# An encoder layer on one core: attention in a written TensorE order by quarters of a head, projections handed out product by product, some normalisations on ScalarE

## The chip, the cores and the metric

The kernel runs on one core of a Trainium2 chip. The time is device microseconds of one execution; the median of three runs of the kernel before is 2068.36 us (2068.29 to 2068.67).

## The reference

Two sequences (`x_prompt`, `x_sample`, here the first and the second stream) of 512 tokens by 1024 channels pass one encoder layer with the same weights: half a SwiGLU feed-forward, a mixing block, another half feed-forward, a last RMSNorm. The mixing block normalises and projects once, runs grouped-query attention and a bidirectional mLSTM side by side, and merges the two by sigmoid gates. What the change touches is the attention and what is computed between its steps:

```python
proj = h @ w_in
aq = apply_rope(rms_norm(aq.reshape(B, S, ATT_HEADS, ATT_HEAD_DIM), q_norm), cos, sin)
ak = apply_rope(rms_norm(ak.reshape(B, S, ATT_KV_HEADS, ATT_HEAD_DIM), k_norm), cos, sin)
...
s = jnp.einsum('bqkgd,bskd->bkgqs', qi, k, preferred_element_type=jnp.float32) * scale
p = jax.nn.softmax(s, axis=-1).astype(v.dtype)
return jnp.einsum('bkgqs,bskd->bqkgd', p, v)
...
merged = jax.nn.sigmoid(g_att) * (att @ w_up_att) + jax.nn.sigmoid(g_mlstm) * (mem @ w_up_mlstm)
```

There are 8 heads of 64 channels, 2 key and value heads, and blocks of 128 queries, so a head has four blocks (0 to 3).

## The kernel before, in words

All of it is float32, made of two float32r halves (a rounded high part and a remainder): a product is three TensorE matmuls (high by high, high by low, low by high) of 128x128 weights by 512 columns. Instructions are recorded in program order; a scheduler then sets the order on each engine from priorities and its own reckoning of when operands are ready, and writes the semaphores. Each engine then runs its list strictly in that order. A few instructions are pinned: they keep the order in which they were recorded (`pin`).

The first feed-forward comes first, then the mixing of both streams (`mix`, a generator that is advanced alternately for the two), then the second feed-forward. In `mix`, `tok_proj` makes keys, values and gates (`kv_done`) and queries (`q_done`), with four PSUM banks at a time: three of the pool MM and the one of PO. `rope_apply` rotates keys and queries on VectorE (DVE); its product with the sine is done in two halves, one for even and one for odd elements (L820). Then follows the attention, head by head:

- `scores(h)`: for each query block, two matmuls into a bank of PS (two banks; L1017), the row maximum on DVE (TENSOR_REDUCE, L1020), the exponential with its row sum on ScalarE (ACT, L1022), a reciprocal and a multiplication of the 128x512 block by it on DVE (L1023, L1024).
- `attend(h)`: for each block of keys, four TensorE transposes into a bank of PT (two banks; L1036), a split into high part (ACT) and remainder (DVE, L671 and L672), and two matmuls with the values into the one bank of PO (L1044); at the end of the head the two halves of PO are added (L1052, L1053).

`scores(h + 1)` is recorded ahead of `attend(h)`. After each head, `fill` hands out one or two units of other work: a projection of 24 matmuls (`proj`, L770), the eight gates of the attention (`att_gate`) and two gates of the mLSTM (`out_gate`), with the load of the next unit's weights ahead of it. In the first stream a weight is split on arrival (L238 on ACT, L239 on DVE) and parked in HBM; in the second stream it comes back split. Each unit ends with a multiplication on DVE and a Tanh on ACT (L1061, L1062). One projection of the mLSTM (`mem_qk(1, 1)`, 24 matmuls) is still held when the attention starts. `extra`, a column sum and a broadcast for the other stream's norm (L202, L212), is recorded once after the third head.

## Time and profile before

| | us |
|---|---|
| median of three runs | 2068.36 |
| the profiled execution, its own time | 2070.33 |
| its span (first to last instruction) | 2068.5 |
| TensorE matmul (PE) busy | 2055.0 |
| TensorE weight load (PEld) busy | 1689.1 |
| VectorE (DVE) busy | 1544.2 |
| ScalarE (ACT) busy | 903.6 |
| GpSimd (POOL) busy | 100.8 |

A record of a matmul lasts from its issue to its modelled end and overlaps the next one, so PE looks busy through short waits. They are found in two other ways: by the number of matmuls in a stretch against the pace of an undisturbed one, and by the idle time of the weight loader, whose records don't overlap. PE is held by a wait at the weight load of the instruction that waits.

### The profile page before, as it was taken

What the parts mean: (1) busy time and instruction counts of PE and PEld (TensorE: products, weight loads), DVE (VectorE), ACT (ScalarE), POOL (GpSimd) and SP (SyncE); (2) the same over time, 40 slices, a digit from 0 to 9 for tenths busy, and PEclk for the clock granted to TensorE, in tenths of its full rate; (3) what the DMA queues carried; (4) which work ended last, traced back from release to release, by engine and by line L of the source; (5) the groups of instructions that cost most, each with busy time, mean ns of one, the idle gap of its engine ahead of it and who ended that gap; (6) DMA issues with size and microseconds to landing.
All of it is one profiled execution on the core that took longest, in us unless ns stands there. A gap on an engine that the chain in (4) does not pass through costs nothing.

```text
span 2068.5 us, 27129 instructions
## 1 busy us (share of the span) xinstructions
PE 2055.0 (99%) x9453; PEld 1689.1 (82%) x9453; DVE 1544.2 (75%) x2784; ACT 903.6 (44%) x1650; POOL 100.8 (5%) x117
## 2 busy tenths in 40 slices
PE   9999999999999999999999999999999999999998
PEld 7888888888888777888877788888888888888887
DVE  7888988786797897575567646545888888795797
ACT  7544444442235566463345443324544444443224
POOL 0000000001003001000120000002000000000001
PEclk9999999999999999999999999999999999999999
DMA  9565655699766645767684345677656555599753
GB/s 323 175 195 172 223 171 185 203 351 347 263 228 248 202 151 186 261 231 271 204 286 162 106 150 190 205 250 249 203 172 215 187 180 183 178 338 355 271 204 120
DMA packets 307240, 454.84 MB, mean 220 GB/s; under 512 B 19976, under 2 KB 179808, under 8 KB 305824
## 3 DMA queue, kind: packets, MB, share of 16 engines
q1 hardware_dynamic: 305104, 447.39, 64.1%
q0 software_dynamic: 1840, 5.46, 0.8%
q8 instruction: 74, 1.21, 0.2%
q14 instruction: 62, 0.51, 0.1%
q10 hardware_dynamic: 160, 0.27, 0.0%
HBM read 286.15 MB, written 166.89 MB: 219 GB/s over the span
## 4 chain that ended last, share of the span: by engine, by line
PE 96%; DVE 1%; DMA 1%; ACT 1%; issue 0%; SPq 0%; ACTq 0%; DVEq 0%
PE mm L770 20%; PE pst L332 12%; PE pso L332 12%; PE mm L332 10%; PE mm L588 8%; PE pss L332 6%; PE pss L588 4%; PE pst L588 4%; PE mm L754 4%; PE pso L588 3%; PE pso L1044 1%; PE pss L1017 1%; PE pso L754 1%; PE pst L1036 1%; PE pso L1180 1%; PE pst L770 1%
## 5 line engine op out<-in xcount | busy, mean ns | idle before, releaser
L770 PE MATMUL mm<-xh,w 128*128 128x512 f32 x896 | 290.4, 394 | 0.0
L332 PE MATMUL pst<-xc,w 128*128 128x512 f32 x1056 | 253.9, 389 | 0.0
L332 PE MATMUL mm<-xc,w 128*128 128x512 f32 x984 | 233.0, 390 | 1.0 <-ACT f L1383 1.0
L332 PEld LDWEIGHTS pst<-xc,w 128*128 128x128 f32 x1056 | 198.0, 188 | 41.7 <-ACT t L367 0.6
L332 PEld LDWEIGHTS mm<-xc,w 128*128 128x128 f32 x984 | 184.2, 188 | 39.4 <-ACT f L1383 1.4
L770 PEld LDWEIGHTS mm<-xh,w 128*128 128x128 f32 x896 | 167.7, 188 | 33.5
L588 PE MATMUL mm<-rt,w 128*128 128x512 f32 x765 | 178.8, 389 | 0.0
L770 PE MATMUL mm<-xl,w 128*128 128x512 f32 x448 | 176.3, 393 | 0.0
L588 PEld LDWEIGHTS mm<-rt,w 128*128 128x128 f32 x765 | 143.6, 188 | 29.8
L290 ACT ACTIVATE w<-t 128x512 fp32r<-128x512 f32 x176 | 107.3, 629 | 135.5 <-issue 55.2
L291 DVE TENSOR_TENSOR w<-t,w 128x512 fp32r<-128x512 f32 x176 | 118.5, 689 | 53.3 <-ACT w L290 51.2
L332 PE MATMUL pso<-xc,f 128*128 128x512 f32 x528 | 126.8, 389 | 0.0
L332 PE MATMUL pss<-xc,w 128*128 128x512 f32 x528 | 126.8, 389 | 0.0
L332 PE MATMUL pso<-xc,w 128*128 128x512 f32 x528 | 126.8, 389 | 0.0
L332 PEld LDWEIGHTS pso<-xc,f 128*128 128x128 f32 x528 | 99.1, 188 | 20.6
L332 PEld LDWEIGHTS pss<-xc,w 128*128 128x128 f32 x528 | 99.1, 188 | 20.6
L332 PEld LDWEIGHTS pso<-xc,w 128*128 128x128 f32 x528 | 99.1, 188 | 20.6
L671 ACT ACTIVATE w<-wr 128x512 fp32r<-128x512 f32 x72 | 45.2, 634 | 138.1 <-PE pso L588 70.2
L671 ACT ACTIVATE w<-t 128x512 fp32r<-128x512 f32 x82 | 51.9, 634 | 107.2 <-PE pst L588 62.4
L770 PEld LDWEIGHTS mm<-xl,w 128*128 128x128 f32 x448 | 84.3, 188 | 16.7
L588 PE MATMUL pss<-rt,w 128*128 128x512 f32 x396 | 93.7, 389 | 0.0
L588 PE MATMUL pst<-rt,w 128*128 128x512 f32 x396 | 93.7, 389 | 0.0
(385 smaller groups left out, 3818.0 us busy)
## 6 DMA issues: line engine op xcount, KB each, us to landing
rt<-rbuf SPq DMA_DIRECT2D x154, 512.0 KB, 5.7
wpark<-w SPq DMA_DIRECT2D x104, 512.0 KB, 3.5
w<-wpark SPq DMA_DIRECT2D x104, 512.0 KB, 4.6
wr<-in_ffn_w_gate_dram SPq DMA_DIRECT2D x62, 512.0 KB, 5.3
rbuf<-tab SPq DMA_DIRECT2D x102, 256.0 KB, 4.0
wr<-in_ffn_w_up_dram SPq DMA_DIRECT2D x44, 512.0 KB, 4.4
rbuf<-f SPq DMA_DIRECT2D x72, 256.0 KB, 4.0
wr<-in_w_in_dram SPq DMA_DIRECT2D x36, 512.0 KB, 5.8
```

Of the source, the lines that this page charges most:

```text
L290: pin(nc.scalar.activation(t[:, 0], src, AF.Copy))
L291: pin(V_.tensor_tensor(t[:, 1], src, f(t[:, 0]), op=ALU.subtract))
L332: nc.tensor.matmul(p, a[:, k, :], xt[:, b, k, :], start=(first and k == 0 and i == 0), stop=(k == HK_ - 1 and i == 2), skip_group_check=True)
L588: nc.tensor.matmul(p, u[:, a, d * P:(d + 1) * P], r[:, b, ts], start=(first and q == 0 and k == 0), stop=(q == len(us) - 1 and k == 2), sk ...
L671: nc.scalar.activation(hi, src, AF.Copy)
L754: nc.tensor.matmul(p[b][:, :N], a[:, k, bs], w_[:, kl, :], start=(k == 0 and i == 0), stop=(k == KD - 1 and i == 2))
L770: nc.tensor.matmul(p, a[:, k, :], b, start=(k == 0 and i == 0), stop=(k == n - 1 and i == 2))
L1017: nc.tensor.matmul(p, qT[:, h, b * P:(b + 1) * P], kv[:, hk * 2 + j, :], start=(j == 0), stop=(j == 1))
L1036: nc.tensor.transpose(p[:, b * P:(b + 1) * P], Ps[b][:, kb * P:(kb + 1) * P], ident)
L1044: nc.tensor.matmul(po, Vst[:, kv_, hk, :], w, start=(kv_ == 0 and i == 0), stop=(kv_ == 3 and i == 1))
L1180: nc.tensor.matmul(po, vm[:, a, t, hs_], b, start=(t == 0 and n == 0), stop=(t == 3 and n == 2))
```

## The change

- The attention is written as quarters of a head. In each quarter TensorE gets: the two score matmuls of one block of the next head, 5 filler matmuls, the four transposes of one key block, 3 filler matmuls, the two value matmuls of the key block before. All are pinned, so TensorE keeps this order; instructions that are not pinned may still stand between them.
- The projections are handed out matmul by matmul (`steps`, `among`) and not in units of 24. The first head's four scores have 9 fillers each. The ten units of the queue hold 240 matmuls; in the first stream the held projection is worked off ahead of the attention (`fill(1)`), in the second it is the first filler, which makes 264. At the end, what is left of the queue is done as before.
- In the first stream, the multiplication by the reciprocal goes to ACT for the odd blocks, 16 in all.
- The sine product of `rope_apply` is one instruction over a reversed pair, no longer two.
- `tok_proj` gets its banks as an argument: PS, PS, MM, MM for keys and values, MM, PO, MM, MM for queries.
- `extra` is split in two: column sums in the third head, broadcast in the fourth.

```diff
     def proj(view, key, src, n, done):
-        return (lambda: load_w(view, key)), (lambda w: done(proj_w(*w, src, n)))
+        def comp(w):
+            done(proj_w(*w, src, n))
+        def steps(w):
...
+                pin(nc.tensor.matmul(p[0], a[:, k, :], b, start=(k == 0 and i == 0), stop=(k == n - 1 and i == 2)))
+                if k == n - 1 and i == 2:
+                    done(p[0])
+            return [lambda k=k, i=i: step(k, i) for k in range(n) for i in range(3)]
...
+    FILLER = 5,3
+    FIRST = 9
...
-                for e in range(2):
-                    V_.tensor_tensor(v5(m)[:, bb, :, :, e], v5(n)[:, bb, :, :, 1 - e],
-                                     s4[:, bb, :, e].unsqueeze(1).to_broadcast([P, hn_, DA // 2]), op=ALU.mult)
+                V_.tensor_tensor(v5(m)[:, bb], v5(n)[:, bb, :, :, ::-1],
+                                 s4[:, bb].unsqueeze(1).to_broadcast([P, hn_, DA // 2, 2]), op=ALU.mult)
...
-        go(*tok_proj(xh, xl, [(512, 256), (2304, 16)], 2, kv_done))
+        go(*tok_proj(xh, xl, [(512, 256), (2304, 16)], 2, kv_done, (PS, PS, MM, MM)))
...
-        go(*tok_proj(xh, xl, [(0, 512)], 2, q_done), mem_qk(0, 0))
+        go(*tok_proj(xh, xl, [(0, 512)], 2, q_done, (MM, PO, MM, MM)), mem_qk(0, 0))
...
+        def score(h, b):
...
+                pin(nc.tensor.matmul(p, qT[:, h, b * P:(b + 1) * P], kv[:, hk * 2 + j, :],
+                                     start=(j == 0), stop=(j == 1)))
...
+            if b % 2 and not s:
+                nc.scalar.activation(e, e, AF.Copy, scale=c[:, 2:3])
+            else:
+                V_.tensor_scalar(e, e, c[:, 2:3], None, op0=ALU.mult)
...
+        def among(n):
+            for _ in range(n):
+                if not between:
+                    if not held:
+                        return
+                    c, w = held.pop(0)
+                    if queue:
+                        load, c2 = queue.pop(0)
+                        held.append((c2, load()))
+                    between.extend(c.steps(w))
+                between.pop(0)()
...
-        Ps = scores(0)
+        if not s:
+            fill(1)
+        Ps = []
+        for b in range(4):
+            Ps.append(score(0, b))
+            among(FIRST)
+        last = None
         for h in range(HA):
-            nxt = scores(h + 1) if h + 1 < HA else None
-            attend(h, Ps)
+            nxt = []
+            for b in range(4):
+                if h + 1 < HA:
+                    nxt.append(score(h + 1, b))
+                among(FILLER[0])
+                pp = turn_keys(Ps, b)
+                among(FILLER[1])
+                if last:
+                    values(*last)
+                last = h, b, pp
+                if extra and b == 2 and h in (2, 3):
+                    extra[h - 2]()
             Ps = nxt
-            fill(1 if h < 4 else 2)
-            if h == 2 and extra:
-                extra()
+        among(FILLER[0])
+        values(*last)
+        among(len(between))
         mem_scales()
         fill(99)
```

In the changed kernel the lines are numbered anew: scores are L1033, filler matmuls L774, transposes L1049, values L1060, the maximum L1036, the reciprocal L1039, the multiplication L1043 (DVE) and L1041 (ACT); `tok_proj` stays L754, and the mLSTM's own scores, L1130 before, are L1179.

TensorE in the first stream, around the end of head 0 before (pss are scores, pst transposes, pso values):

```order
L1036 MATMUL pst_6114<-ident,t_510_5960 128x128
L1036 MATMUL pst_6114<-ident,t_513_5969 128x128
L1017 MATMUL pss_6095<-kv_5250,qT_5253 128x512 x2
L1044 MATMUL pso_5991<-t_532_6029,kv_5250 128x512
L1017 MATMUL pss_6104<-kv_5250,qT_5253 128x512 x2
L1036 MATMUL pst_6114<-ident,t_516_5978 128x128
L1036 MATMUL pst_6114<-ident,t_519_5987 128x128
L1036 MATMUL pst_6123<-ident,t_510_5960 128x128
```

Two score blocks stand one value matmul apart, inside one group of transposes. The same engine and place now, one quarter of head 0:

```order
L1033 MATMUL pss_6134<-kv_5250,qT_5253 128x512 x2
L774 MATMUL mm_6089<-xh_4859,w_6012 128x512
L774 MATMUL mm_6089<-xl_4860,w_6012 128x512
L774 MATMUL mm_6089<-xh_4859,w_6012 128x512 x2
L774 MATMUL mm_6089<-xl_4860,w_6012 128x512
L1049 MATMUL pst_6148<-ident,t_503_5953 128x128
L1049 MATMUL pst_6148<-ident,t_510_5980 128x128
L1049 MATMUL pst_6148<-ident,t_513_5998 128x128
L1049 MATMUL pst_6148<-ident,t_520_6027 128x128
L774 MATMUL mm_6089<-xh_4859,w_6012 128x512 x2
L774 MATMUL mm_6089<-xl_4860,w_6012 128x512
L1060 MATMUL pso_6103<-t_542_6125,kv_5250 128x512
```

Scores, transposes and values now stand apart by fillers, and the scores of the next block come a whole quarter later.

DVE now, in the quarter in which a projection ends (first stream, end of head 0; mm_6089 is the projection, w_6179 a weight split for a later one):

```order
L1036 TENSOR_REDUCE asm_6165<-pss_6162 128x1
L1094 TENSOR_TENSOR mg_5910<-mm_6089,R_5126 128x512
L1039 RECIPROCAL asm_6165<-asm_6165 128x1
L1043 TENSOR_SCALAR t_552_6167<-t_552_6167,asm_6165 128x512
L239 TENSOR_TENSOR w_6179<-wr_6177,w_6179 128x1024
L672 TENSOR_TENSOR t_559_6193<-pst_6187,t_558_6192 128x512
L1072 TENSOR_TENSOR f_560_6201<-pso_6103,f_561_6202 64x512
```

and before, the corresponding stretch:

```order
L1053 TENSOR_TENSOR f_533_6036<-pso_5991,f_534_6037 64x512
L942 TENSOR_TENSOR f_539_6073<-mm_6048,R_5126 128x512
L1023 RECIPROCAL asm_6098<-asm_6098 128x1
L1023 RECIPROCAL asm_6107<-asm_6107 128x1
L239 TENSOR_TENSOR w_6285<-wr_6283,w_6285 128x1024
L672 TENSOR_TENSOR qk_5912<-f_539_6073,qk_5912 128x512
L1024 TENSOR_SCALAR t_548_6100<-t_548_6100,asm_6098 128x512
L1024 TENSOR_SCALAR t_551_6109<-t_551_6109,asm_6107 128x512
L672 TENSOR_TENSOR t_555_6120<-pst_6114,t_554_6119 128x512
```

Two blocks' reciprocals and multiplications stood together before; now there is one block per quarter, and the odd blocks' multiplication is not on DVE.

TensorE now, where the fillers of the first stream have run out (head 6, with the scores of head 7):

```order
L1049 MATMUL pst_6903<-ident,t_717_6831 128x128
L754 MATMUL mm_7114<-w_7100,xh_4859 128x512 x2
L1060 MATMUL pso_6912<-t_725_6873,kv_5250 128x512
L1060 MATMUL pso_6912<-t_726_6874,kv_5250 128x512
L1033 MATMUL pss_6915<-kv_5250,qT_5253 128x512 x2
L1049 MATMUL pst_6924<-ident,t_695_6738 128x128
L1049 MATMUL pst_6924<-ident,t_703_6770 128x128
L1049 MATMUL pst_6924<-ident,t_710_6799 128x128
L1049 MATMUL pst_6924<-ident,t_717_6831 128x128
L1060 MATMUL pso_6912<-t_732_6908,kv_5250 128x512
L754 MATMUL mm_7114<-w_7100,xl_4860 128x512
L1060 MATMUL pso_6912<-t_733_6909,kv_5250 128x512
```

The scheduler puts matmuls of the mLSTM's values (L754) and scores (L1179), which are not pinned, between the pinned ones: 19 and 6 from the last filler to the last value matmul of the first stream. Before, the last head of that stream stands among projections:

```order
L1036 MATMUL pst_6951<-ident,t_724_6817 128x128
L1130 MATMUL pss_7012<-qk_5837 128x512 x3
L1130 MATMUL pss_7025<-qk_5837 128x512 x3
L1044 MATMUL pso_6941<-t_750_6947,kv_5250 128x512
L770 MATMUL mm_7086<-xh_4859,w_6907 128x512
L770 MATMUL mm_7086<-xl_4860,w_6907 128x512
L770 MATMUL mm_7086<-xh_4859,w_6907 128x512
L1036 MATMUL pst_6962<-ident,t_715_6790 128x128
```

What moved is the other work that stands beside the last head: projections before, the mLSTM's work now. Ahead of the mixing of the first stream, and from the end of the second stream's attention on, the order on TensorE is the same but for buffer numbers and a few rows; the number of matmuls and transposes is the same in both kernels.

More of the change, by code (lines that the diff above doesn't have):

```diff
@@ new lines, in score, with turn_keys, values @@
+            return e
+        def turn_keys(Ps, kb):
+            p = PT()
+            for b in range(4):
+                pin(nc.tensor.transpose(p[:, b * P:(b + 1) * P], Ps[b][:, kb * P:(kb + 1) * P], ident))
+            ph, pl = T2(F32R), T2(F32R)
+            split(p, ph, pl)
+            return ph, pl
+        pos = {}
+        def values(h, kb, pp):
+            if kb == 0:
+                pos[h] = PO()
+            for i, w in enumerate(pp):
+                pin(nc.tensor.matmul(pos[h], Vst[:, kb, h // 4, :], w, start=(kb == 0 and i == 0),
+                                     stop=(kb == 3 and i == 1)))
+            if kb < 3:
+                return
+            po = pos.pop(h)
```

71 lines of the change are left out of this document (34 added, 37 removed).

## The prediction

> **What bounds the kernel now.** I read the page's totals first.
>
> ```profile
> span 2068.5 us, 27129 instructions
> PE 2055.0 (99%) x9453; PEld 1689.1 (82%) x9453; DVE 1544.2 (75%) x2784; ACT 903.6 (44%) x1650; POOL 100.8 (5%) x117
> PE 96%; DVE 1%; DMA 1%; ACT 1%; issue 0%; SPq 0%; ACTq 0%; DVEq 0%
> ```
>
> TensorE sets the time. The change neither adds nor removes a matmul, so it can give back only the time in which TensorE stands still. Since records of PE overlap, I take its pace from the chain of work and its counts from windows over the two attentions; the last two rows are the same windows for the transposes alone.
>
> ```profile
> 439.23 6.12 PE mm L588 x27
> 792.12 0.88 PE pst L1036 x8
> 705.48:826.75 121.27, 120.36 (x591) 94.72 (x590) 103.43 (x214) 77.90 (x165) 7.95 (x6) 1.00 0.51 167
> 1094.71:1209.22 114.51, 114.14 (x558) 90.61 (x557) 83.60 (x190) 61.48 (x143) 1.07 (x2) 1.00 0.35 114
> 705.48:826.75 121.27, 22.68 (x152) 18.00 (x152) 0.00 (x0) 1.00 0.51 167
> 1094.71:1209.22 114.51, 20.59 (x136) 15.71 (x136) 0.00 (x0) 1.00 0.35 114
> ```
>
> An undisturbed 512-column matmul takes 6.12 / 27 = 0.227 us, a transpose 0.88 / 8 = 0.11. The first attention holds 591 - 152 = 439 matmuls and 152 transposes: 99.5 + 16.7 = 116.2 of its 121.27 us, so **5.0 us** are lost. The second holds 422 and 136: 95.7 + 15.0 = 110.6 of 114.51, **3.9 us** lost. What the loss is, the waits of the weight loader tell (us in total, times, longest), first window, then second:
>
> ```profile
> PEld pss L1017 <- ACT t L1022: 3.3, 11, 0.6
> PEld pst L1036 <- DVE t L672: 1.6, 3, 1.0
> PEld pso L1044 <- ACT t L671: 1.6, 5, 0.5
> PEld pso L1044 <- DVE t L672: 1.1, 5, 0.3
> ...
> PEld pst L1036 <- DVE t L672: 2.3, 8, 0.6
> PEld pss L1017 <- ACT t L1022: 2.0, 5, 0.7
> ```
>
> Scores wait for a PS bank whose exponential isn't done, values for their split, transposes for a PT bank. One of them in the timeline:
>
> ```profile
> 721.72 0.69 ACT L1022 ACTIVATE t<-pss,asm 128x512 f32<-128x512 f32 x1 [2.17 <-DVE asm L1020]
> 722.55 0.30 PEld L1017 LDWEIGHTS pss<-kv,qT 128*128 128x128 f32 x2 [0.36 <-ACT t L1022]
> ```
>
> The score matmul starts 0.14 us after the exponential that held its bank (721.72 + 0.69): it was recorded too close behind. These are short waits of operands that come just late, not an engine that is full: DVE is busy 103.43 of 121.27 us (85%), ACT 64%.
>
> **The change, part by part.** Durations of one instruction in the first attention (mean ns after the comma):
>
> ```profile
> L1020 DVE TENSOR_REDUCE asm<-pss 128x1 f32<-128x512 f32 x32 | 21.7, 685 | 0.8 <-PE pss L1017 0.4
> L672 DVE TENSOR_TENSOR t<-pst,t 128x512 fp32r<-128x512 f32 x28 | 18.9, 687 | 3.8 <-ACT t L671 2.4 <-PE pso L1044 1.1 <-PE pst L1036 0.2
> L1024 DVE TENSOR_SCALAR t<-t,asm 128x512 f32<-128x512 f32 x32 | 16.3, 517 | 0.5
> L239 DVE TENSOR_TENSOR w<-wr,w 128x1024 fp32r<-128x1024 f32 x10 | 12.2, 1217 | 0.5 <-ACT w L238 0.3
> L1061 DVE TENSOR_TENSOR mg<-mm,R 128x512 f32<-128x512 f32 x8 | 5.5, 686 | 1.0 <-PE mm L770 1.0
> L1023 DVE RECIPROCAL asm<-asm 128x1 f32<-128x1 f32 x32 | 4.8, 157 | 1.1 <-ACT t L1022 0.9
> L1053 DVE TENSOR_TENSOR f<-pso,f 64x512 f32<-64x512 f32 x6 | 4.1, 688 | 2.1 <-ACT f L1052 1.8
> L820 DVE TENSOR_TENSOR t<-t,tab 128x256 f32<-128x256 f32 x4 | 1.5, 423 | 0.0
> L815 DVE TENSOR_TENSOR t<-t,tab 128x512 f32<-128x512 f32 x2 | 1.4, 690 | 0.0
> ...
> L1022 ACT ACTIVATE t<-pss,asm 128x512 f32<-128x512 f32 x32 | 21.8, 687 | 7.0 <-DVE asm L1020 5.3 <-DVE asm L1023 1.4
> L671 ACT ACTIVATE t<-pst 128x512 fp32r<-128x512 f32 x28 | 16.3, 595 | 10.2 <-PE pso L1044 5.2 <-PE pst L1036 4.9
> L238 ACT ACTIVATE w<-wr 128x1024 fp32r<-128x1024 f32 x10 | 10.6, 1060 | 7.4 <-PE mm L770 7.4
> L1022 ACT ACTIVATION_READ_ACCUMULATOR t<-pss,asm 128x1 f32 x32 | 6.3, 197 | 0.0
> L1062 ACT ACTIVATE mg<-mg 128x512 f32<-128x512 f32 x8 | 5.0, 624 | 1.8 <-DVE mg L1061 1.8
> L671 ACT ACTIVATE att<-f 128x512 fp32r<-128x512 f32 x3 | 1.9, 634 | 1.0 <-DVE f L1053 1.0
> ```
>
> A quarter on TensorE is 12 matmuls and 4 transposes: 2.72 + 0.44 = 3.16 us. Beside it DVE has, per quarter, maximum, reciprocal, split and half a multiplication (0.685 + 0.157 + 0.687 + 0.26), a third of a unit's end (1.217 + 0.686) and about a quarter of a head's end (0.688, and 0.686 in every second): 2.7 us, 85%; with all multiplications it would be 2.9. ACT has 2.6. So neither is the bound, and what counts is whether each operand is there when its turn comes.
>
> Scores of block 3 to the next head's first transposes: 17 matmuls and 4 transposes, 4.3 us. The chain between is 0.685 + 0.687 + 0.197 + 0.157, a split in front on ACT 0.595, the multiplication on ACT 0.634 (the nearest row is the 128x512 copy att<-f): 2.96. It fits with 1.3 to spare.
>
> Transposes to their values: 15 matmuls and 4 transposes, 3.84 us; the chain is 0.595 + 0.687 = 1.28. In the quarter where a unit ends, DVE runs in front of the split, by the order shown, a gate's multiplication, a reciprocal, a multiplication and a weight's remainder: 0.686 + 0.157 + 0.517 + 1.217 + 0.687 = 3.26 from the unit's last matmul, which is 2.6 after the transposes' end. PO's addition, which frees the bank for the next head, follows at 3.3: 0.5 to spare.
>
> Scores use a PS bank every second quarter, 6.3 us apart. **So in the steady quarters none of the rows above should wait.**
>
> Where waits remain: (1) The first head of the first stream. A gate's multiplication, a reciprocal, a multiplication and a weight's remainder (2.58 us from the unit's end, which is 5 matmuls, 1.13 us, before the end of block 3's scores) stand ahead of block 3's maximum, and the next head's first exponential ahead of its multiplication: 1.45 + 0.685 + 0.884 + 0.884 + 0.634 = 4.5 us after its scores it is ready, and it is wanted after 3.96 (16 matmuls, 3 transposes). With the restart of the loader I take 0.8 us. (2) The fillers run out. The first four scores take 36, each quarter 8, so 240 last 25.5 quarters and 264 in the second stream 28.5, of 32. In the first stream 25 matmuls of the mLSTM are laid into the last 6.5 quarters, so a quarter there is 1.35 us of attention and 0.87 of those, 2.2, against DVE's 2.05 (the sum above without a unit's end): following the rows I find three waits of a quarter to a third of a microsecond, 0.9 us together, and give the second stream the same. (3) 0.5 for hand-overs that I don't see. Together 3.1 us of the 8.9: **5.8 gained**. The bounds: 8.9 if none waits, and below, the rivals.
>
> The banks: the waits at the start of the projections of keys and queries, first stream; the second stream has the first row once more.
>
> ```profile
> PEld mm L754 <- DVE kv L835: 0.5, 2, 0.4
> PEld pso L754 <- DVE xs L621: 0.2, 1, 0.2
> ```
>
> That is 1.2 us for both. Queries now begin on two banks that no one holds, but reach keys' last banks after 7 matmuls, 1.6 us, about when they come free: I take half, **0.6** (0 to 1.2).
>
> The sine product: two instructions of 0.423 or one of between 0.69 (L815, the same size) and 1.22 (L239, twice the elements, if a reversed step cost double); I take 0.69. Eight per stream, less than 1.3 us won or 3.0 lost on DVE for the stream, hidden behind the projections that TensorE has while the queries are rotated (24 matmuls each) and the 36 fillers: nothing. Multiplications on ACT: 16 of 0.634 for 0.517, inside the spare 1.3: nothing; without that cover 16 x 0.117 = 1.9 us. The DMAs are those of before, a unit's load one unit ahead: a unit now lasts three quarters, 9.5 us. The split `extra` puts its transposes between quarters, each with a PT bank that was freed a quarter before: nothing.
>
> Here a rule of the Trainium skill speaks against the change: "ScalarE: Activation LUTs", "Rules for kernel authors", sends multiplications to VectorE, not ScalarE. The rows agree on the instruction (0.634 against 0.517); by the rule the sum would be 4.5 us and not 6.4. "Perfetto Trace Analysis", "Optimizing Scalar/DVE Operations", allows the move where VectorE is saturated, which 85% is not quite.
>
> The sum is 5.8 + 0.6 = **6.4 us** off the profiled execution's 2070.33 (span 2068.5 and 1.8 around it). That execution is 0.1% over the median of the runs, 2068.36; taken off the median, **2062.0**.
>
> **The rivals.** (a) *The waits move to the end.* For: the fillers cover 25.5 and 28.5 quarters of 32. If the mLSTM's matmuls can't stand in, since their weights come late, each of ten quarters takes DVE's 2.05 and not 1.35: 7 us in place of the 1.8 I gave. The gain is then 1.2, **2067.2**. Against: the order has those matmuls there. (b) *The fixed order waits everywhere, slower.* Pinned, TensorE may not pass a late operand, and the fillers behind it wait too. The place is the split of the transposes, which in the first stream queues behind weights on ACT and DVE. If each of the 64 quarters has one wait of the mean size of the scores' row, 3.3 / 11 = 0.3 us, that is 19.2 in place of 8.9: 2068.36 + 10.3 - 0.6, **2078**. It decides from 0.15 us per quarter on. Against: 0.5 to 1.3 us to spare in each chain worked out above. (c) *ACT's multiplications lie on the path*, the rule just named: 1.9 us less gained, **2063.9**. That the change doesn't do what it says I exclude: the pinned quarters stand in the order as written.
>
> **How the numbers follow.** Measurements of this kernel can tell about 0.2%, 4.1 us: faster is under 2064.2, slower over 2072.5. My forecast has 0.56, (c) 0.04, (a) and other near draws 0.25, (b) 0.15. So faster 0.60, same 0.25, slower 0.15. The range begins where every wait is gone, 2068.36 - 8.9 - 1.2 = 2058.3, and reaches over (a) to 2070; it leaves out (b) and a twentieth.
>
> **What would show it.** In the loader's waits over both attentions, the scores' wait for the exponential should be gone or under 0.5 us, those for the splits under 2; matmuls and transposes at their pace should fill all but 3 us of the two stretches. Waits of the first transposes of a head for ACT's multiplication would speak for (c); waits in the last seven quarters, for the split or the scores, for (a); a wait at values or transposes in most quarters for (b). At the keys' and queries' start the two waits should halve. I'd be wrong if an engine's list, not TensorE's, held a late instruction in front of many others: ACT idle before a weight's high part, with the exponentials behind it.

## The result, and the profile after

The changed kernel takes 2064.61 us (median of 18 runs, 2063.55 to 2067.25), beside 2068.93 us for the kernel before (18 runs, 2067.6 to 2072.0): ratio 0.998, 95% interval 0.9974 to 0.9987. That is **4.3 us faster** (2.7 to 5.4 by the interval); 6.4 were forecast. The profiled execution took 2063.99 us.

Three lines of its page, as before: span, busy times, and the engines' shares of the chain that ended last.

```profile
span 2062.2 us, 27043 instructions
PE 2049.4 (99%) x9453; PEld 1692.5 (82%) x9453; DVE 1542.4 (75%) x2752; ACT 913.1 (44%) x1666; POOL 100.4 (5%) x117
PE 97%; ACT 1%; DVE 1%; DMA 1%; issue 0%; SPq 0%; ACTq 0%; DVEq 0%
```

The totals say almost nothing: 9453 matmuls and transposes again, PE at 99% again. The answer lies in the two attentions. The windows hold the same work as those of the prediction; a third one covers nine quarters (score, fillers, transposes, fillers, values) of the second stream. The counts in brackets take in records that only reach over a window's edge: from start to start the third window holds 108 matmuls and 36 transposes. First all instructions, then the transposes alone.

```profile
703.79:823.21 119.42, 118.09 (x591) 96.42 (x590) 93.50 (x181) 83.02 (x169) 4.46 (x4) 1.00 0.50 166
1090.95:1202.96 112.01, 111.99 (x559) 92.25 (x557) 84.05 (x175) 58.85 (x129) 1.38 (x2) 1.00 0.36 120
1108.33:1137.13 28.80, 28.80 (x146) 23.89 (x145) 21.59 (x43) 15.41 (x35) 0.00 (x0) 1.00 0.33 109
```

```profile
703.79:823.21 119.42, 22.93 (x152) 18.57 (x152) 0.00 (x0) 1.00 0.50 166
1090.95:1202.96 112.01, 20.36 (x136) 16.89 (x136) 0.00 (x0) 1.00 0.36 120
1108.33:1137.13 28.80, 5.39 (x36) 4.49 (x36) 0.00 (x0) 1.00 0.33 109
```

The first attention went from 121.27 to 119.42 us, the second from 114.51 to 112.01: 1.85 + 2.5 = 4.35 us. At the forecast's pace (116.2 and 110.6 us) 3.2 and 1.4 are still lost, 4.6 of the 8.9. Who waits there, the weight loader's list tells: first attention, then second (us in total, times, longest).

```profile
PEld pst L1049 <- DVE t L672: 1.0, 1, 1.0
PEld pst L1049 <- ACT t L1041: 1.0, 1, 1.0
PEld pso L1060 <- DVE t L672: 0.7, 3, 0.3
```

```profile
PEld pso L1060 <- DVE f L1072: 0.5, 1, 0.5
PEld pso L1060 <- DVE t L672: 0.2, 1, 0.2
```

The scores' waits for the exponential (3.3 and 2.0 us before) are gone from both. Two waits of 1 us are left in the first attention, and small ones where the fillers run out. In the window of nine quarters the list is empty, and still a quarter takes 28.80 / 9 = 3.20 us, not the 3.16 that 12 matmuls at 0.227 and 4 transposes at 0.11 make. **A quarter of this mixed stream costs 0.04 us more than its count says, with nobody waiting.** The starts of four rows of one such quarter show that no one place has it:

```profile
1111.88 0.62 PE L1033 MATMUL pss<-kv,qT 128*128 128x512 f32 x2
1113.48 0.60 PE L1049 MATMUL pst<-ident,t 128*128 128x128 f32 x4
1114.38 0.40 PE L774 MATMUL mm<-xl,w 128*128 128x512 f32 x1
1115.07 0.39 PE L1033 MATMUL pss<-kv,qT 128*128 128x512 f32 x1
```

Two scores and five fillers take 1.60 us (1.59 by the count), four transposes and two fillers 0.90 (0.89), a filler and two values 0.69 (0.68).

With this the waits can be told from the rest. I take the time from each start on TensorE to the next, subtract the pace (0.227 us for a matmul, 0.109 for a transpose, and 0.343 for a set's last transpose with the matmul behind it), and call what exceeds it by 0.03 us or more in one step TensorE **standing still**. In the windows of the two attentions it stood for 4.2 and 2.9 us before, 7.1 together, and stands for 2.2 and 0.3 now, 2.5. The smaller excesses are 2.3 us before and 2.5 now: both kernels have them.

The keys' and queries' start of the first stream; the second stream has the same row:

```profile
PEld mm L754 <- DVE kv L853: 0.3, 1, 0.3
```

Before, 0.5 and 0.2 stood there, and 0.5 in the second stream. From the first product of the keys to the first of those windows the trace has 55.87 us and had 56.49: 0.6 less. So the two profiled executions differ by 6.3 us in time, and the places named account for some 5. Another 1.1 us lie ahead of the keys (their first product started at 647.92 us, before at 648.99), where both programs are the same: single executions differ by about this much, and the medians are what counts.

The two waits that are left, in the timeline. First the first transposes of the attention, those of the first head; the expectations below call them the second head's, but they turn the blocks of head 0. (Start, duration, engine, and in brackets the wait.)

```profile
723.53 0.69 ACT L1038 ACTIVATE t<-pss,asm 128x512 f32<-128x512 f32 x1 [0.52 <-DVE asm L1036]
724.21 0.71 ACT L1041 ACTIVATE t<-t,asm 128x512 f32<-128x512 f32 x1
724.97 0.14 PEld L1049 LDWEIGHTS pst<-ident,t 128*128 128x128 f32 x1 [0.98 <-ACT t L1041]
```

ScalarE multiplies the first head's block 3 only after the next head's first exponential; this is the forecast's first remaining wait, 0.8 us, and TensorE stands for 0.9. The other was not forecast. It lies in the third head, behind the first transposes of `extra`:

```profile
755.95 2.64 POOL L1006 TENSOR_TENSOR box<-box,tab 128x512 f32<-128x512 f32 x2 [92.23 <-issue]
757.30 1.58 DVE L1043 TENSOR_SCALAR t<-t,asm 128x512 f32<-128x512 f32 x1
758.80 1.21 DVE L239 TENSOR_TENSOR w<-wr,w 128x1024 fp32r<-128x1024 f32 x1
759.93 0.68 DVE L672 TENSOR_TENSOR t<-pst,t 128x512 fp32r<-128x512 f32 x1
760.66 0.42 PEld L1049 LDWEIGHTS pst<-ident,t 128*128 128x128 f32 x4 [1.03 <-DVE t L672]
```

`extra` took a PT bank, so the next transposes need the bank of the quarter just before. Its split (759.93) stands on VectorE behind a multiplication that took 1.58 us in place of 0.5 and behind a weight's remainder. TensorE stands still for 0.77 us.

### The profile page after: what moved, and what is told of

Same layout as the page of the kernel before. It is cut to its first block, busy times and chain, and to the rows that moved or that the text cites. A ratio compares the mean times of both kernels' runs of the same rounds, so it can differ in the third digit from the quotient of the medians.

```text
span 2062.2 us, 27043 instructions
## 1 busy us (share of the span) xinstructions
PE 2049.4 (99%) x9453; PEld 1692.5 (82%) x9453; DVE 1542.4 (75%) x2752; ACT 913.1 (44%) x1666; POOL 100.4 (5%) x117
## 4 chain that ended last, share of the span: by engine, by line
PE 97%; ACT 1%; DVE 1%; DMA 1%; issue 0%; SPq 0%; ACTq 0%; DVEq 0%
PE mm L787 16%; PE pst L332 12%; PE pso L332 12%; PE mm L332 11%; PE mm L588 8%; PE pss L332 6%; PE mm L774 5%; PE pst L588 4%; PE pss L588 4%; PE mm L754 4%; PE pso L588 3%; PE pso L1060 1%; PE pss L1033 1%; PE pst L1049 1%; PE pso L1229 1%; PE pss L1179 1%
## 5 line engine op out<-in xcount | busy, mean ns | idle before, releaser
L588 PE MATMUL mm<-rt,w 128*128 128x512 f32 x765 | 178.8, 389 | 0.0
L588 PEld LDWEIGHTS mm<-rt,w 128*128 128x128 f32 x765 | 143.6, 188 | 29.7
L787 PEld LDWEIGHTS mm<-xh,w 128*128 128x128 f32 x560 | 104.9, 188 | 21.1
L774 PE MATMUL mm<-xh,w 128*128 128x512 f32 x336 | 114.6, 401 | 0.0
L787 PE MATMUL mm<-xl,w 128*128 128x512 f32 x280 | 109.7, 392 | 0.0
L588 PE MATMUL pst<-rt,w 128*128 128x512 f32 x396 | 93.7, 389 | 0.0
L588 PE MATMUL pss<-rt,w 128*128 128x512 f32 x396 | 93.6, 389 | 0.0
```

The costliest lines, as they stand in the source:

```text
L588: nc.tensor.matmul(p, u[:, a, d * P:(d + 1) * P], r[:, b, ts], start=(first and q == 0 and k == 0), stop=(q == len(us) - 1 and k == 2), sk ...
L774: pin(nc.tensor.matmul(p[0], a[:, k, :], b, start=(k == 0 and i == 0), stop=(k == n - 1 and i == 2)))
L787: nc.tensor.matmul(p, a[:, k, :], b, start=(k == 0 and i == 0), stop=(k == n - 1 and i == 2))
```

## Experiments

The theory: the gain comes from the order that the change writes, scores one block at a time with fillers between, which gives each operand time to be ready. Rivals: the bank lists carry it; the relief of VectorE (the multiplications on ScalarE and the sine product in one instruction) carries it; the pinning carries it. No run has the new order without the bank lists or without the new sine product. Then come runs on the two waits, and on how many fillers a quarter needs. All are timed beside the kernel before; a ratio has its 95% interval. The third column is measured in the profiled execution from the first of the keys' products in the first stream to the start of a later stage that no kernel alters (L588 for the second time, at 1837.6 us in the changed kernel); it leaves the part ahead of the keys out. The fourth and fifth are how long TensorE stands still in that execution, as defined above, from 700 to 830 us (first attention) and from 1088 to 1215 us (second).

| kernel | median us | trace us | stands, first | stands, second | ratio to before |
|---|---|---|---|---|---|
| before | 2068.93 | 1194.9 | 4.4 | 2.9 | |
| changed | 2064.61 | 1189.7 | 2.3 | 0.3 | 0.998 (0.9974 to 0.9987) |
| without pins | 2063.04 | 1188.6 | 1.4 | 0.4 | 0.9971 (0.9959 to 0.9982) |
| before, banks alone | 2067.74 | 1193.8 | 4.0 | 3.3 | 0.9996 (0.9987 to 1.0005) |
| before, relief alone | 2067.18 | 1192.0 | 2.5 | 2.4 | 0.9992 (0.9983 to 1.0001) |
| all on VectorE | 2064.84 | 1190.2 | 2.6 | 0.4 | 0.998 (0.9971 to 0.9989) |
| sums at b == 0 | 2064.96 | 1190.2 | 3.0 | 0.3 | 0.9983 (0.9974 to 0.9992) |
| first head on VectorE | 2064.03 | 1188.5 | 1.5 | 0.4 | 0.9978 (0.9969 to 0.9987) |
| three fillers | 2093.44 | 1218.0 | 18.7 | 13.3 | 1.0121 (1.0107 to 1.0135) |
| box on VectorE | 2064.65 | 1190.9 | 1.8 | 0.4 | 0.9982 (0.9973 to 0.9991) |
| sums at b == 3 | 2064.33 | 1189.3 | 2.1 | 0.3 | 0.998 (0.9971 to 0.9989) |
| no pins, b == 3, first head | 2063.28 | 1187.7 | 0.9 | 0.3 | 0.9975 (0.9965 to 0.9985) |
| seven fillers | 2068.14 | 1193.2 | 5.9 | 0.4 | 0.9999 (0.9991 to 1.0008) |
| nine fillers | 2064.19 | 1189.4 | 2.6 | 0.3 | 0.9979 (0.997 to 0.9988) |

The last two columns already say where which part works. In the second attention, which has no multiplication on ScalarE, every kernel in the new order with seven fillers or more stands for 0.3 to 0.4 us, and the old order for 2.4 to 3.3, with or without the other parts: there the order alone takes the waits away. (That 2.9 and 3.3 come from the same instructions in that stretch shows how far single executions differ.) In the first attention the order with all multiplications on VectorE goes from 4.4 to 2.6, and the relief alone in the old order goes to 2.5: either does there nearly what both do together, 2.3.

### The order without the pins

```diff
-    pin(nc.tensor.transpose(p[:, b * P:(b + 1) * P], Ps[b][:, kb * P:(kb + 1) * P], ident))
+    nc.tensor.transpose(p[:, b * P:(b + 1) * P], Ps[b][:, kb * P:(kb + 1) * P], ident)
```

and so for the scores, the values and the fillers.

> The changed kernel with the same recorded order in quarters, but without the pins: the scheduler may again move TensorE's instructions. If the order of recording (one block of scores, fillers, one set of transposes, fillers, values) is what takes the short waits away, the time stays within 1 us of the changed kernel's 2064.6 and the weight loader's waits over the two attentions stay near its 3.8 us. If the pinning itself is what gains, because the scheduler moves matmuls to places where their operands are late, the time goes back towards the kernel before, 2067 or more. If the pinning costs (a late operand cannot be passed by), it comes out 0.5 to 1 us faster than the changed kernel, with the waits at the second head's first transposes (0.9 us) and in the third head (0.8 us) gone.

Measured: 2063.04 us, 1.6 faster than the changed kernel by the medians, a little past the fast side of the expectation (the ranges of the runs overlap: 2062.62 to 2063.9 beside 2063.55 to 2067.25). The whole gain is kept: **the recorded order does it, not the pinning**. Of the two waits that should have gone, one did, nearly. At the first head's first transposes of this kernel:

```profile
724.68 0.71 ACT L1041 ACTIVATE t<-t,asm 128x512 f32<-128x512 f32 x1
725.45 0.14 PEld L1049 LDWEIGHTS pst<-ident,t 128*128 128x128 f32 x1 [0.24 <-ACT t L1041]
```

ScalarE's multiplication ends as late as before, but the scheduler has put three fillers and a score's first matmul ahead of the fourth transpose, and 0.24 us of waiting is left of 0.98. The wait in the third head stayed (0.78 us on TensorE). The trace has about 1 us of difference, 0.9 of it in the first attention; the rest I did not locate.

### The bank lists alone

```diff
-        go(*tok_proj(xh, xl, [(0, 512)], 2, q_done), mem_qk(0, 0))
+        go(*tok_proj(xh, xl, [(0, 512)], 2, q_done, (MM, PO, MM, MM)), mem_qk(0, 0))
```

and the keys' list, in the kernel before.

> The kernel before with the bank lists of the keys' and queries' projections alone. My theory of the banks: the waits at the start of keys and queries, about 1.2 us in both streams, shrink by about 0.7 us as they did in the changed kernel (0.73 to 0.25 us and 0.46 to 0.18 us), and nothing else changes: 0.7 us faster than the kernel before, about 2068.2. The rival, that the banks carry most of the gain: 3 us or more faster. The other rival, that the bank held is only waited for a little later: no difference, under 0.2 us.

Measured: 1.0 us under the median of before (2068.71 beside it), 1.1 in the trace. The interval reaches over 1, so the time alone is inconclusive, but in the first stream the queries' wait is down from 0.5 to 0.3 us and the keys' 0.2 is gone, as after the change. From the first product of the keys to the first score the first stream is 0.4 us shorter; the rest of the 1.1 I did not locate. The size agrees with mine of 0.7, and the rival with 3 us falls.

### The relief of VectorE alone, in the old order

```diff
-                V_.tensor_scalar(e, e, c[:, 2:3], None, op0=ALU.mult)
+                if b % 2 and not s:
+                    nc.scalar.activation(e, e, AF.Copy, scale=c[:, 2:3])
+                else:
+                    V_.tensor_scalar(e, e, c[:, 2:3], None, op0=ALU.mult)
```

and the sine product in one instruction, in the kernel before.

> The kernel before, in its old order of whole heads, with the odd blocks' multiplications of the first stream on ScalarE and the sine product in one instruction. My theory: VectorE was not the bound (85% busy in the first attention), the late operands come from the order in which whole heads are recorded, so this gives little: between 1 us faster and 1 us slower than the kernel before (16 multiplications of 0.634 us put in front of the exponentials on ScalarE, 16 of 0.517 taken from VectorE). The rival, that relief of VectorE carries the gain: 2 us or more faster, with the first attention's wait for splits and scores halved and the second attention's unchanged.

Measured: 1.5 us under before, more than I expected, less than the rival. The loader's waits of the first attention:

```profile
PEld pss L1016 <- ACT t L1021: 1.6, 7, 0.3
PEld pst L1038 <- DVE t L672: 0.8, 3, 0.3
```

They were 3.3 and 1.6. (In the second attention, which has no multiplication on ScalarE, the scores' wait is 1.5 and was 2.0; it was 2.4 with the bank lists alone, so 0.5 is within what executions differ by.) So about half the scores' wait of the first attention in the old order hung on VectorE's list, although that engine was busy for only 85% of the window; that a late multiplication there holds the next maximum, and this the exponential, is argued, not shown. Which of the two edits does it wasn't tried. The interval of the ratio reaches over 1, so the 1.5 us rests on the medians and on the trace, which has 2.9.

### All multiplications on VectorE, in the new order

```diff
-            if b % 2 and not s:
+            if False:
```

> The changed kernel with all multiplications by the reciprocal on VectorE. My theory: in the steady quarters neither place is on the path, so only the start of the first attention changes: the wait of the second head's first transposes for ScalarE's multiplication (0.9 us) becomes one for VectorE's, a little later or earlier (the wait 0.5 to 1.5 us), and the time is within 1 us of the changed kernel. The rule that multiplications belong on VectorE would make it 1 to 2 us faster. If VectorE's relief is what the first attention needs (2.9 us per quarter of 3.16 with all multiplications), it is 2 us or more slower, with waits for splits in most unit's ends.

Measured: 2064.84 us, 0.2 slower than the changed kernel; the time is as forecast. But not because nothing changes:

```profile
PEld pso L1060 <- DVE f L1072: 1.4, 3, 0.7
PEld pst L1049 <- DVE cs L204: 0.7, 1, 0.7
PEld pst L1049 <- DVE t L1043: 0.6, 2, 0.5
```

The wait at the first head is gone (0.08 us left, where 0.5 to 1.5 was expected). In its place values wait for PO's addition, which stands on VectorE, and in the third head two sets of transposes wait, one for the column sums and one for a multiplication. On TensorE 0.9 and 0.77 us have become 0.26, 0.45, 0.42 and 0.40. **The move to ScalarE is worth nothing in the new order; in the old one the relief, which is this move and the sine product, gave 1.5 us.**

### The column sums after the first quarter

```diff
-                if extra and b == 2 and h in (2, 3):
+                if extra and b == 0 and h in (2, 3):
```

> The changed kernel with the column sums (extra) laid in after the first quarter of a head, b == 0, and not after the third, b == 2. My theory: their transposes take a PT bank, so that the next quarter's transposes need the bank of the quarter just before, and at b == 2 of the third head that quarter is also the end of a unit, whose weight's remainder (1.21 us) stands ahead of the split on VectorE; that gave the wait of 0.77 us there. At b == 0 no unit ends, and the wait goes: 0.6 to 0.9 us faster than the changed kernel. The rival, that the late split comes from the multiplication by the reciprocal alone (1.58 us in place of 0.5, while GpSimd adds the box), wherever the sums stand: no difference, since the slowed multiplication holds up another transpose or value.

Measured: 2064.96 us, 0.35 over the changed kernel and not 0.6 to 0.9 under it: the rival's time. The transposes' wait went, and a larger one came (one matmul of the values stands for 1.46 us):

```profile
756.18 1.20 DVE L191 SCALAR_TENSOR_TENSOR rs<-rs,rs 128x4 f32<-128x4 f32 x1
757.91 0.86 DVE L188 SCALAR_TENSOR_TENSOR rs<-rs 128x4 f32<-128x4 f32 x1
760.03 1.21 DVE L239 TENSOR_TENSOR w<-wr,w 128x1024 fp32r<-128x1024 f32 x1
763.17 0.19 PEld L1060 LDWEIGHTS pso<-t,kv 128*128 128x128 f32 x1 [1.73 <-DVE t L672]
```

The statistics behind the sums are a dozen 128x4 instructions of 0.15 us each; at b == 0 they are mixed into the quarter in which a unit ends, ahead of its split. And two of them took 1.20 and 0.86 us while GpSimd added its box (756.07 to 758.74 us): as the rival has it, what GpSimd holds up is only another instruction, here 1.8 us on VectorE just ahead of the unit's end.

### The first head's multiplications on VectorE

```diff
-            if b % 2 and not s:
+            if b % 2 and not s and h:
```

> The changed kernel with the multiplications of the first stream's first head all on VectorE; later heads' odd blocks stay on ScalarE. My theory: the wait of the second head's first transposes for ScalarE's multiplication (0.9 us, forecast at 0.8) goes, as in the run with all multiplications on VectorE, where 0.08 us was left, and nothing comes in its place: 0.7 to 0.9 us faster than the changed kernel. The rival, that VectorE then runs late through the next unit's end: the same time, with a new wait of 0.3 us or more before 745 us.

Measured: 2064.03 us, 0.6 less than the changed kernel, a little under what was expected, and not clear of noise by the medians alone; in the first attention of the trace it is 0.7. The row of L1041 is gone from the loader's list, 0.07 us of standing is left there, and no new wait of 0.3 us is there. The theory holds. The third head's wait is as it was, at 760.71 us, although here the multiplication is not slow: now the weight's remainder is, 2.22 us in place of 1.22.

### Three fillers in a quarter

```diff
-    FILLER = 5,3
+    FILLER = 2,1
```

> The changed kernel with three fillers in a quarter, not eight; the rest of the fillers runs behind the last head. My theory: the fillers are what gives each chain its time. A quarter on TensorE is then 4 + 3 matmuls and 4 transposes, 1.59 + 0.44 = 2.03 us, and VectorE needs 0.685 + 0.157 + 0.687 + 0.26 + 0.26 and an eighth of 1.9, 2.3 us, in the first stream and 2.5 in the second: waits of 0.25 to 0.5 us in each of 32 quarters, 8 us in the first and 11 to 15 in the second attention, so 10 to 25 us slower than the changed kernel, spread over all heads. The rival, that only the order counts and not how much lies between: within 2 us of the changed kernel.

Measured: 2093.44 us, 28.8 slower: beyond my range, and far from the rival. A window from the middle of the first attention, and the waits of the whole of it:

```profile
735.00:785.00 50.00, 40.27 (x200) 30.11 (x200) 40.13 (x89) 35.55 (x75) 2.53 (x2) 1.00 0.33 103
```

```profile
PEld pst L1049 <- ACT t L1041: 10.2, 7, 2.6
PEld pso L1060 <- DVE t L672: 4.9, 10, 1.0
PEld pso L1060 <- DVE f L1072: 4.3, 7, 1.7
```

TensorE stands 13 us longer in the second attention, as expected, but 16.4 in the first, where 8 was expected. My price went by VectorE's work per quarter, but VectorE is busy for 40.13 of 50 us, and ScalarE for 35.55. No engine is full. What lacks is time along the chain (maximum, exponential, reciprocal, multiplication, transposes, split), so the estimate by engine was too low there.

### The box addition on VectorE

```diff
-            (G_, V_)[s].tensor_tensor(em3, eb3, tabs[3][:, d].unsqueeze(1).to_broadcast([P, 4, P]), op=ALU.add)
+            V_.tensor_tensor(em3, eb3, tabs[3][:, d].unsqueeze(1).to_broadcast([P, 4, P]), op=ALU.add)
```

> The changed kernel with the box addition of the first stream's memory rows on VectorE, as it is in the second, so that GpSimd does nothing beside the attention. Theory of the port: the multiplication at 757.3 us took 1.58 us and not 0.5 because GpSimd's addition (2.64 us for two) ran beside it; without it every multiplication takes 0.5 to 0.55 us, and the wait of 0.77 us in the third head shrinks to 0.3 or less: up to 0.5 us faster than the changed kernel. The rival, that the slow multiplication has another cause (its data, its place): one of 1.4 us or more is there again. VectorE gets 0.69 us more for each addition, and where it waits there for the box to arrive, the splits behind it are late: then up to 2 us slower.

The instructions of VectorE at the place of the slow multiplication, and the wait behind them:

```profile
757.77 0.67 DVE L1006 TENSOR_TENSOR box<-box,tab 128x512 f32<-128x512 f32 x1
759.53 0.48 DVE L1043 TENSOR_SCALAR t<-t,asm 128x512 f32<-128x512 f32 x1
```

```profile
PEld pst L1049 <- DVE t L672: 0.4, 1, 0.4
```

The multiplication takes 0.48 us again, though an addition now stands on the same engine, and TensorE waits 0.17 us in place of 0.77: **0.6 of the 0.77 us came from GpSimd's addition beside it**. The median is that of the changed kernel, 2064.65: the trace, which is of the slowest of this kernel's executions, shows nearly 2 us more in what follows the first attention, and I did not follow it further.

### The column sums after the fourth quarter

The edit is that of b == 0, with b == 3.

> The changed kernel with the column sums laid in after the fourth quarter of a head, b == 3. The run with b == 0 showed that the bank is not all: there the first wait went, and the many small instructions of the statistics then stood between the splits on VectorE beside a unit's end, which made values wait 1.46 us. At b == 3 the sums come one quarter after the unit's end, when the late split is done, so by the theory of the bank the wait of 0.77 us goes, and the small instructions fall into quarters 12 and 13, of which the second ends a unit: 0 to 0.5 us of new waits there. So 0.2 to 0.8 us faster than the changed kernel. The rival, that the slow multiplication beside GpSimd's addition (0.6 of the 0.77 us by the run with the box on VectorE) makes a wait wherever the sums stand: no difference.

Measured: 2064.33 us, 0.3 less than the changed kernel, which the time alone can't separate from it. In the list of the first attention:

```profile
PEld pst L1049 <- DVE t L672: 0.3, 1, 0.3
PEld pso L1060 <- DVE f L1072: 0.8, 2, 0.7
```

The transposes' wait shrinks from 1.0 to 0.3, and 0.4 us of it come back on TensorE at 781.43 us, at PO's addition. The multiplication beside GpSimd's addition was held up here too, 1.40 us, and no transposes waited behind it. So the 0.77 us took both, the bank that the sums had taken and the addition, and either edit removes most of that wait.

### The three together

Without pins, with b == 3, and the first head on VectorE.

> The changed kernel without the pins, with the column sums after the fourth quarter, and the first head's multiplications on VectorE. The run without pins was 1.5 us faster than the changed kernel, and kept the wait of 0.8 us in the third head; the second head's wait is gone there already. If the gains add: 2061.9 to 2062.9, the fastest here. The rival, that without pins the scheduler fills the hole at the third head with something else already or moves the sums' transposes anyway: the 2063.0 of the run without pins.

Measured: 2063.28 us, the rival's result; the gains don't add in the time. In the trace it is the fastest by 0.8 us, with these left of the two waits:

```profile
PEld pst L1049 <- DVE t L672: 0.6, 2, 0.4
PEld pso L1060 <- ACT t L671: 0.4, 2, 0.2
```

Whether it is faster than the order without pins (2062.62 to 2063.9; here 2062.6 to 2063.83) stays open.

### Seven fillers in a quarter

```diff
-    FILLER = 5,3
+    FILLER = 4,3
```

> The changed kernel with seven fillers in a quarter, so that 204 behind the first four scores last 29 quarters of the first stream and 228 all 32 of the second. Theory of the tail: the waits where the fillers run out (0.3 us in the first, 0.4 us in the second attention) shrink by half; but a quarter is 2.93 us against VectorE's 2.7 to 2.9 with a unit's end in every 3.4 quarters, so chains with 0.5 us to spare keep 0.3: within 0.5 us of the changed kernel, either sign. The rival, that eight fillers are at the edge of what the chains need: 1.5 us or more slower, with waits at unit's ends all along.

Measured: 2068.14 us, 3.5 slower: the rival's result, and nearly the whole gain is lost. It is the first attention alone:

```profile
PEld pso L1060 <- DVE f L1072: 3.2, 3, 1.9
PEld pst L1049 <- ACT t L1041: 2.4, 2, 1.2
```

```profile
766.12 0.48 DVE L1043 TENSOR_SCALAR t<-t,asm 128x512 f32<-128x512 f32 x1
766.51 0.68 DVE L1072 TENSOR_TENSOR f<-pso,f 64x512 f32<-64x512 f32 x1
767.24 0.30 PEld L1060 LDWEIGHTS pso<-t,kv 128*128 128x128 f32 x2 [1.87 <-DVE f L1072]
```

The next head's first values wait for the addition that frees the one PO bank, and on VectorE that stands behind a weight's remainder, three of the small instructions of the statistics, two maxima, a split and a multiplication. The second attention, in which weights come split and no remainder is in the list, lost nothing.

### Nine fillers in a quarter

The edit is that of seven, with 6,3.

> The changed kernel with nine fillers in a quarter. With three it was 29 us slower and with seven 3.5 us. If eight is already past the edge (the waits left in the changed kernel come from the first head, the column sums and the end, none from a chain that is too short), nine takes no wait away in the steady quarters and lengthens the end without fillers from 6.5 to 9 quarters in the first and from 3.5 to 6.5 in the second attention, at some 0.1 us of wait a quarter: 0 to 0.7 us slower than the changed kernel. If eight is still short of the edge, the waits at the second head's first transposes (0.9 us) and at the column sums (0.8 us) shrink by 0.23 us each, one more matmul's time, and it is about 0.5 us faster.

Measured: 2064.19 us, 0.4 less than the changed kernel, within what the runs can tell apart. The list of its first attention begins:

```profile
PEld pst L1049 <- ACT t L1041: 1.3, 3, 0.7
PEld pso L1060 <- DVE f L1072: 0.8, 3, 0.3
```

The first head's wait shrank by 0.23 us on TensorE, as the second reading has it, and small waits came at the end, as the first has it. At the column sums nothing is left, but 0.29 us came at the broadcast (776.95 us); GpSimd's two additions stand 8 us apart here, so this place isn't a clean comparison. Nine does not drift back as seven does, although with nine, too, a unit's end falls on changing places in a head; which speaks for the time in a quarter, and not the rhythm, as what seven lacks.

## Why the prediction was right, and where its size was off

*The bound and the mechanism: right.* TensorE's share and count didn't change, the short waits went, and in nine steady quarters nothing waits. Most of the signs set down came: the scores' wait for the exponential is gone, the splits' waits are 1.9 us in all (forecast: under 2), and the keys' and queries' waits are about half. One did not: the two stretches should have been filled at their pace but for 3 us, and 4.6 are left. That the gain is the order's doing is shown from both sides: without the pins it stays, and with fewer fillers it turns to a loss. In the second attention no other part does anything that stands out of the scatter; in the first the relief alone, in the old order, took away nearly as much.

*"8.9 lost, 3.1 of it remains, 5.8 gained": right in kind, off in size.* Gained were 4.35 in the profiled executions, and 4.6 of the 8.9 remained. The prediction took the whole difference from the pace for waits ("What the loss is, the waits of the weight loader tell"). The loss was even a little larger, 9.6 us, since its counts take in two matmuls of the first window and one of the second that only reach over the edge or begin at it. But TensorE stood still for only 7.1 of that; nearly all the rest are the small excesses of the mixed stream, 2.3 us, which the changed kernel has as well (2.5). Of the 7.1 us of waits 2.5 remain, *fewer* than the 3.1 forecast. A stretch of the kernel before in which nothing waits would have given the floor.

*The remaining waits.* The first head: 0.8 forecast, 0.9 measured, by the chain described, and removed by its own edit. The ends: 0.9 for each stream forecast; TensorE stands for 0.25 in the first and 0.33 in the second. The loader's lists show more, 0.7 us in three waits of the first, but a wait of 0.2 to 0.3 us of the loader is one of 0.1 or less in TensorE's starts here. The half microsecond for what I didn't see: it was the 0.77 at `extra`, and that it nearly fits is luck.

*"The split `extra` puts its transposes between quarters, each with a PT bank that was freed a quarter before: nothing."* Wrong. The bank was claimed by the next transposes while its split was late, 0.77 us; GpSimd's addition, which no step of mine had looked at, made 0.6 of it. Rows of the kernel before did show it: a 0.77 us wait of transposes at 745.33 us, behind this multiplication at 1.59 us while GpSimd added.

*The banks: 0.6 forecast for both streams.* Right, or a little low: 0.6 from the keys' first product to the attention in the first stream's trace alone, 1.0 by the run with them alone. *The sine product at nothing.* Its worth wasn't measured alone. Its price is as taken: one instruction of 128x512 now takes what L815 took, 0.69 us, for two of 0.42:

```profile
L838 DVE TENSOR_TENSOR t<-t,tab 128x512 f32<-128x512 f32 x8 | 5.5, 682 | 0.0
```

*ScalarE's multiplications at nothing.* Right in the sum, and each took 0.715 us rather than 0.634:

```profile
L1041 ACT ACTIVATE t<-t,asm 128x512 f32<-128x512 f32 x16 | 11.4, 715 | 0.7 <-DVE asm L1039 0.7
```

In this the Trainium skill's rule ("ScalarE: Activation LUTs", "Rules for kernel authors") is right on the instruction, 0.715 against 0.5, and didn't decide: with all of them on VectorE the kernel is 0.2 us slower, so rival (c) falls. It must be judged by that run, for the time itself, 2064.61, lies nearer to (c)'s 2063.9 than to the forecast's 2062.0, and the sign set down for (c), a head's first transposes waiting for ScalarE's multiplication, did come once, at the first head.

*The rivals.* (a), waits at the end: not seen at more than 0.33 us in either stream. (b), the fixed order waits everywhere: not at eight fillers, but the run with seven, 0.23 us less in a quarter, is at 2068.14, and with three it is slower by far. The prediction counted 0.5 to 1.3 us to spare in each chain; where a unit's end meets a head's end there must have been less. The pins, for which the sum had no term at eight fillers, cost 1.6 us by the medians and about 1 by the traces.

Of the 2.6 us between 2062.0 and 2064.61, 0.6 is the starting point, since 18 runs put the kernel before at 2068.93 and not 2068.36, and 1.45 is what the attentions gained less. The last 0.6 is open: the difference of medians, 4.3, is 0.7 below the 5 located in single executions. The median is also 0.4 short of the prediction's own mark for a gain that measurements can tell, 2064.2; with 18 runs of each kernel, the interval of the ratio lies below 1 all the same.

## What to carry to other kernels

A matmul engine at 99% can still hold some microseconds of short waits; lay independent products between the producer and the consumer of each operand, and count how long the chain is, not how busy its engines are: seven products in a quarter lost what eight had gained. Before calling lost time waiting, take the pace of the mixed instruction stream from a stretch in which the wait list is empty. A relief of a helper engine is worth what the order makes it worth: moving multiplications off VectorE gave nothing in the new order, and together with the new sine product 1.5 us in the old one.

## What the hardware showed that I had not expected

A VectorE instruction that starts while GpSimd adds two SBUF tensors can wait for it and show that as its own duration. In the changed kernel the multiplication at 757.30 us took 1.58 us (0.48 when GpSimd was idle), and GpSimd's second addition ended at 755.95 + 2.64 = 758.59. It is the place, not the operation: without the pins the same addition made the weight's remainder 2.23 us long, with the first head on VectorE 2.22, both in place of 1.22; and with the sums at b == 0 an instruction of only 128x4 took 1.20 us in place of 0.15, so what is paid is about the rest of GpSimd's instruction, however small the one that waits. The instructions beside it that read one operand from PSUM (the splits and the gate's multiplication) kept their 0.68 us. The Trainium skill, "SBUF — State Buffer", "Who interferes with whom", says just this: the two engines lock a shared pair of ports for a whole instruction, a tensor-scalar operation in its fast mode or one with two SBUF inputs contends, and the later one blocks. These traces agree, and put a price on it here: 1.0 to 1.1 us on VectorE for one instruction, and 0.6 on TensorE where a bank hung on it (none with the sums at b == 3).
